# Layer 0 starts with two groups of value columns for each slice of x instead of one

## The chip, the core and the metric

The kernel runs on one core of a Trainium2 chip. The time is that of one execution on the device in microseconds (us); a measurement gives the median of several. Lines such as L313 are lines of the kernel before.

## What is computed

Two layers of a block on x, 256 positions by 2048 features, in float32. Each layer projects x to ten groups of columns (convolution, six hgrn heads, six retention heads), mixes along the sequence in three ways, projects back, adds and normalises, then does a squared-ReLU feed-forward of width 8192, adds and normalises again.

```python
for l in range(DEPTH):
    proj = jnp.einsum('btd,de->bte', x, w_in[l])
    ca, cg, hq, hf, hi, hg, rq, rk, rv, rg = jnp.split(proj, split_idx, axis=-1)
    y_conv = conv_mixer(ca, cg, ...)
    y_hgrn = hgrn2_mixer(hq, hf, hi, hg, lower_bounds[l], hgrn_norm_g[l])
    y_ret = retention_mixer(rq, rk, rv, rg, positions, ...)
    mix = jnp.concatenate([y_conv, y_hgrn, y_ret], axis=-1)
    x = layer_norm(DEEPNORM_ALPHA * x + mix @ w_out[l], ...)
    f = jnp.square(jax.nn.relu(x @ w_ff1[l]))
    x = layer_norm(DEEPNORM_ALPHA * x + f @ w_ff2[l], ...)
```

The values are the columns hi and rv, 768 each: 1536 columns, that is three groups of 512. Heads 0 to 3 of hgrn read group 0; hgrn heads 4 and 5 read the first half of group 1, retention heads 0 and 1 the second half; the other retention heads read group 2.

## The kernel before, in words

Every large product is made of float32r matmuls on numbers split in two: a cast to float32r (the high part) and the remainder. Weights come from HBM in float32 into one of three `raw` buffers of 1 MB (`load2`, L268). ScalarE (ACT) casts half a buffer into a `wp` tile (L288), VectorE (DVE) writes the remainder beside it (L291). Such a half is a *unit*; there are six `wp` tiles. x goes the same way into the `act` tiles (L388, L390).

There are two kinds of product. `xstat` holds a 128x128 block of x in TensorE (PE) and streams 512 weight columns past it (L313): for each of eight slices i of 256 features, two tiles t of 128 positions, with six matmuls each (two blocks of 128 features, three products: high by high, high by remainder, remainder by high). A group so takes 96 matmuls in two PSUM accumulators. `wstat` holds weights and streams x (L363, L365), 256 output columns at a time, in two loads of 1 MB. There are four accumulators, `mm`. The value groups go through `xstat`, the other columns of the input projection through `wstat`, in the order of the table `ORDER`.

Nothing runs in the order in which the code stands. Each operation is handed to a planner (`Plan`) with its engine, a cost, what it reads and writes, and urgency. The planner lays all engines out by its own costs and then emits each engine's fixed sequence. The large products keep their order on PE (`main`); the casts keep the order of the units (chain `hi`), the remainders theirs (chain `lo`), and the weight loads theirs on SyncE's queue (chain `dma`). The rest (products of the heads on PE, evictions, 124 multiply-adds of the convolution on DVE) is put between. On the chip each engine takes its sequence strictly in order, and an instruction that waits holds up what stands behind it. A load into a `raw` buffer waits until the part of the buffer that it writes has been read by the cast and the remainder.

Layer 0 begins with eleven warm-up matmuls on zeros (L449). Then value group 0 runs while x itself arrives: `first_x` loads a transposed slice of x (0.25 MB for each of the first two, then 0.5 MB for two slices together), and splits it. `fine` says into how many parts the load of a 1 MB weight buffer is cut: four for the first, two for the others. After the fourth slice `setup` loads the constants (`cst`), a mask and the positions, and works out tables on DVE and ACT: the lower bounds (`lbs`, L494 to L514), the mask's cast (L460), and the angles (L465 to L484). Then come the `wstat` products from `ORDER`. Value group 1 stands ahead of ("hf", 2), the gates of the third pair of hgrn heads, and value group 2 ahead of ("rq", 0), the first retention pair. The score products of an hgrn pair are L588, seven steps of L604, and L645; the convolution's transposes are L803, its ACT steps L815 and L824, and the product that follows them on DVE L828.

Of the kernel before, what the change touches and what calls it, by code (L numbers as in the profile page):

```python
# [202 lines left out]
def block_kernel(ctx: ExitStack, tc: tile.TileContext, a: dict, out: bass.AP):  # L203
# [7 lines left out]
    def ring(name, n, shape, dt=F32, p=pool):  # L211
        return Ring([p.tile(list(shape), dt, name=f"{name}{i}") for i in range(n)])
# [8 lines left out]
    mm = ring("mm", 4, [P, W], F32, psum)  # L221
# [43 lines left out]
    def load2(src, parts=1):  # L265

        raw, n = raws.buf(), 2048 // parts
        ops = [op("DMA", 2.92 / parts, lambda f=f: nc.sync.dma_start(  # L268
            out=raw.t[:, f * n:(f + 1) * n], in_=src[:, f * n:(f + 1) * n]), w=[(raw, f * n // 1024 if parts == 2
                                                                                else f if parts > 1 else None)],  # L270
            chain="dma") for f in range(parts)]
        return raw, ops, parts

    def unit(ld, i, pool_lo=False):

        u = Unit()
        raw, dmas, parts = ld
        u.w, u.parts = wps.buf(), max(parts // 2, 1)
        n = 1024 // u.parts
        u.ops = dmas[i * u.parts:(i + 1) * u.parts] if parts > 1 else dmas  # L280
        u.ops = [(o, 4.5) for o in u.ops]
        for f in range(u.parts):
            sl, pt = slice(f * n, (f + 1) * n), f if u.parts > 1 else None
            rs = slice(1024 * i + f * n, 1024 * i + (f + 1) * n)
            rk = (raw, None if parts == 1 else i * u.parts + f)

            def hi(sl=sl, rs=rs):
                S.copy(out=u.w.t[:, 0, sl], in_=raw.t[:, rs])  # L288

            def lo(sl=sl, rs=rs):  # L290
                (G if pool_lo else V).tensor_tensor(out=u.w.t[:, 1, sl], in0=raw.t[:, rs],  # L291
                                                    in1=u.w.t[:, 0, sl].bitcast(F32), op=ALU.subtract)

            eng, cost = ("POOL", 2.35) if pool_lo else ("DVE", dve(n))
            u.ops += [(op("ACT", act(n), hi, r=[rk], w=[(u.w, pt)], chain="hi"), 2.5),
                      (op(eng, cost, lo, r=[rk], w=[(u.w, pt)], chain="lo" + eng), 1.3)]
        return u
# [6 lines left out]
    def mmx(u, ps, xT, i, t):  # L304

        parts = u.parts
        for kbs in ((0, 1),) if parts == 1 else ((0,), (1,)):
            def fn(kbs=kbs):
                w = u.w.t.rearrange("p s (k c) -> p s k c", k=2)
                for kb in kbs:  # L310
                    k = 2 * i + kb
                    for n, (xs, ws) in enumerate(((0, 0), (0, 1), (1, 0))):
                        nc.tensor.matmul(  # L313
                            ps.t, lhsT=xT[k // 4].t[:, xs, k % 4, t * P:(t + 1) * P], rhs=w[:, ws, kb, :],
                            start=(k == 0 and n == 0), stop=(k == KB - 1 and n == 2))

            w = u.w if parts == 1 else (u.w, kbs[0])
            needed(u, plan.main(3 * len(kbs) * 0.2161, fn, [w, (xT[i // 2], i if (i // 2, parts) == (0, 2) else t)],
                                [ps]))

    def xstat(src, xT, done, head=0, tail=0, before=None, pool_lo=(), fine={}):

        ps = [mm.buf(), mm.buf()]
        order = [(i, t) for i in range(8) for t in range(2)]
        if tail:
            order = order[:16 - 2 * tail] + [(i, t) for t in range(2) for i in range(8 - tail, 8)]
        if head:
            order = [(i, 0) for i in range(head)] + [(0, 1), (1, 1), (2, 1)]  # L330
            for i in range(head, 8):
                order += [(i, 0), (i - head + 3, 1)]
            order += [(i, 1) for i in range(8) if (i, 1) not in order]
        us = {}
        for i, t in order:
            if t == 0:
                if before is not None:
                    before(i)
                if i % 2 == 0:
                    ld = load2(src[i // 2], fine.get(i, 1))  # L340
                us[i] = unit(ld, i % 2, i in pool_lo)
            mmx(us[i], ps[t], xT, i, t)
            if i == 7:
                done(t, ps[t])

    def wstat(src, xT, dst=None):

# [76 lines left out]
    xT = [acts.buf() for _ in range(4)]  # L424
# [521 lines left out]
    for l in range(DEPTH):  # L946
        mixT = [acts.buf() for _ in range(4)]
        vt = []

        def vgroup(g, **kw):  # L950
            tl = []
            vt.append(tl)

            def done(t, ps):
                v = r2.buf()
                op("ACT", act(W, ps=True), lambda: S.copy(out=v.t, in_=ps.t), r=[ps], w=[v], floor=1.5)
                tl.append(v)

            xstat(a["wv"][l, g], xT, done, **kw)

        if l == 0:
            def before(i):
                first_x(i)
                if i == 3:
                    setup((plan.last["PE"],))

            vgroup(0, before=before, fine={0: 4, 2: 2, 4: 2, 6: 2})
            whole(xT[0])
        else:
            vgroup(0, head=HEAD, pool_lo=POOL_LO)  # L970
            norm.rest()
        pairs, gates = {}, {}
        for i, (kind, p) in enumerate(ORDER):
            if (kind, p) == ("hf", 2):
                vgroup(1)
            if (kind, p) == ("rq", 0):
                vgroup(2)
            if kind in ("hf", "rq"):
                pair = pairbufs.buf()
                pairs[kind[0], p] = pair  # L980
            dst = None
            if kind in ("rq", "rk"):
                dst = (pairs["r", p], "Q" if kind == "rq" else "K", pv(pairs["r", p], 0 if kind == "rq" else 1))
            pr = wstat(a["wp"][l, i], xT, dst)
            if l == 0 and i == 1:
                op("DMA", 6.0, lambda: nc.sync.dma_start(out=x_nat.t, in_=a["x"].rearrange("(t p) d -> p t d", p=P)),
                   w=[x_nat], after=(plan.last["PE"],))
            if kind == "hf":
                hgrn_gates(l, p, pr, pair)
            elif kind == "hq":  # L990
                Qv = pv(pair, 2)
                op("ACT", act(W), lambda Qv=Qv, pr=pr: S.activation(out=Qv(), in_=pr.t, func=AF.Sigmoid), r=[pr],
                   w=[(pair, "Q")])
                op("DVE", dve(W), lambda Qv=Qv, pr=pr: V.tensor_tensor(out=Qv(), in0=pr.t, in1=Qv(), op=ALU.mult),
                   r=[pr], w=[(pair, "Q")])
            elif kind == "hg":
                gate = r2.buf()
                op("ACT", act(W), lambda gate=gate, pr=pr: S.activation(out=gate.t, in_=pr.t, func=AF.Sigmoid),
                   r=[pr], w=[gate])
                hgrn(l, p, pairs["h", p], gate, vt, mixT)  # L1000
            elif kind in ("cg", "ca"):
                def uv(p=p):
                    return u_t.t[:, 2 * p:2 * p + 2, CONVW - 1:]

                uk = [(u_t, 2 * p), (u_t, 2 * p + 1)]
                if kind == "cg":
                    op("ACT", act(W), lambda uv=uv, pr=pr: S.activation(out=uv(), in_=bl(pr.t, 2), func=AF.Sigmoid),
                       r=[pr], w=uk)
                else:
                    op("DVE", dve(W), lambda uv=uv, pr=pr: V.tensor_tensor(out=uv(), in0=bl(pr.t, 2), in1=uv(),  # L1010
                                                                           op=ALU.mult), r=[pr], w=uk)
                    if p == 0:
                        accs = [r2.buf(), r2.buf()]
                    conv_taps(l, accs[p], 2 * p)
                    if p == 1:
                        conv(l, accs, mixT)
            elif kind == "rg":
                gate = r2.buf()
                op("ACT", act(W), lambda gate=gate, pr=pr: S.activation(out=gate.t, in_=pr.t, func=AF.Sigmoid),
                   r=[pr], w=[gate])  # L1020
                op("DVE", dve(W), lambda gate=gate, pr=pr: V.tensor_tensor(out=gate.t, in0=pr.t, in1=gate.t,
                                                                           op=ALU.mult), r=[pr], w=[gate])
                ret(l, p, pairs["r", p], gate, vt, mixT)
# [8 lines left out]
        xT = norm.xT  # L1032
# [37 lines left out]
        xT = norm.xT  # L1070
# [107 lines left out]
```

## Time and profile before

| what | value |
|---|---|
| median of three executions | 2340.0 us (2339.7 to 2341.8) |
| the profiled execution's own time | 2341.0 us |
| its span, first to last instruction | 2339.2 us |
| PE, DVE, ACT busy | 99%, 64%, 45% of the span |
| first matmul of value group 0, first matmul of the first `wstat` | 5.49 us, 32.32 us |

Times in rows of the timeline are us from the first instruction: start, duration, engine, line, operation, out<-in, how many in a row, and in brackets the idle time before with what ended it. In a list of groups a row ends with busy us, mean ns of one, and the idle time ahead of it. A row of a DMA group gives its count, the KB of one and the median us from issue to landing. Matmuls overlap: one is shown as busy for about 0.5 us, and the next begins before it ends.

### The profile page before, as it was taken

What the parts mean: (1) busy time and instruction counts of PE and PEld (TensorE: products, weight loads), DVE (VectorE), ACT (ScalarE), POOL (GpSimd) and SP (SyncE); (2) the same over time, 40 slices, a digit from 0 to 9 for tenths busy, and PEclk for the clock granted to TensorE, in tenths of its full rate; (3) what the DMA queues carried; (4) which work ended last, traced back from release to release, by engine and by line L of the source; (5) the groups of instructions that cost most, each with busy time, mean ns of one, the idle gap of its engine ahead of it and who ended that gap; (6) DMA issues with size and microseconds to landing.
All of it is one profiled execution on the core that took longest, in us unless ns stands there. A gap on an engine that the chain in (4) does not pass through costs nothing.

```text
span 2339.2 us, 29616 instructions
## 1 busy us (share of the span) xinstructions
PE 2320.4 (99%) x12067; PEld 1974.0 (84%) x12067; DVE 1504.0 (64%) x2046; ACT 1054.0 (45%) x1334; POOL 65.0 (3%) x66
## 2 busy tenths in 40 slices
PE   9999999999999999999999999999999999999998
PEld 7888888788888888888888888887888888888886
DVE  6997666665565565565579976656655655655655
ACT  6445444454344344344444455444543444443442
POOL 0000000100000000000000000101000000000000
PEclk9999999999999999999999999999999999999999
DMA  8544566465555555556454445564555555555563
GB/s 299 181 162 162 171 198 207 162 207 188 190 189 189 198 180 198 188 190 205 167 205 162 163 162 174 189 218 159 205 198 185 193 187 191 185 193 198 181 229 113
DMA packets 67705, 439.90 MB, mean 188 GB/s; under 512 B 7664, under 2 KB 7920, under 8 KB 16624
## 3 DMA queue, kind: packets, MB, share of 16 engines
q1 hardware_dynamic: 67568, 438.01, 55.0%
q8 instruction: 94, 1.54, 0.2%
q14 instruction: 43, 0.35, 0.0%
HBM read 432.74 MB, written 2.10 MB: 186 GB/s over the span
## 4 chain that ended last, share of the span: by engine, by line
PE 98%; DVE 1%; DMA 0%; ACT 0%; issue 0%; SPq 0%; DVEq 0%
PE mm L313 44%; PE mm L363 33%; PE mm L365 17%; PE aux L604 2%; PE aux L399 1%; DVE x_nat L889 0%; DMA raw<-in_wv 0%; PE aux L550 0%; PE aux L552 0%; PE aux L588 0%; PE aux L548 0%; PE aux L717 0%; DVE x_nat L883 0%; ACT r L913 0%; DVE sm L861 0%
## 5 line engine op out<-in xcount | busy, mean ns | idle before, releaser
L291 DVE TENSOR_TENSOR wp<-raw,wp 128x1024 fp32r<-128x1024 f32 (+1 forms) x796 | 970.9, 1221 | 602.4 <-ACT wp L288 600.6
L288 ACT CAST wp<-raw 128x1024 fp32r<-128x1024 f32 (+1 forms) x802 | 842.4, 1052 | 819.0 <-PE mm L313 561.7
L363 PE MATMUL mm<-act,wp 128*128 128x512 f32 x3328 | 1180.8, 399 | 0.0
L313 PE MATMUL mm<-wp,act 128*128 128x512 f32 x4608 | 1061.1, 390 | 3.9 <-ACT wp L288 1.7
L313 PEld LDWEIGHTS mm<-wp,act 128*128 128x128 f32 x4608 | 861.1, 188 | 185.4 <-ACT wp L288 2.9
L365 PE MATMUL mm<-act,wp 128*128 128x256 f32 x3328 | 933.2, 280 | 0.0
L363 PEld LDWEIGHTS mm<-act,wp 128*128 128x128 f32 x3328 | 625.4, 188 | 151.5
L365 PEld LDWEIGHTS mm<-act,wp 128*128 128x128 f32 x3328 | 628.4, 189 | 0.5
L372 ACT COPY r<-mm 128x256 f32<-128x256 f32 x208 | 77.9, 375 | 369.6 <-PE mm L365 369.3
L375 DVE TENSOR_TENSOR r<-mm,r 128x256 f32<-128x256 f32 x184 | 78.1, 424 | 146.2 <-ACT r L372 145.9
L791 DVE SCALAR_TENSOR_TENSOR r<-u_t,cst,r 128x256 f32<-128x256 f32 x240 | 102.1, 479 | 0.0
L407 POOL TENSOR_TENSOR sm<-sm,mhalf 128x4 f32<-128x4 f32 (+1 forms) x24 | 30.4, 1266 | 2252.5 <-DVE sm L873 1589.4
L388 ACT CAST act<-r 128x512 fp32r<-128x512 f32 x82 | 51.5, 628 | 21.7 <-DVE r L1049 16.2
L390 DVE TENSOR_TENSOR act<-r,act 128x512 fp32r<-128x512 f32 x82 | 57.9, 706 | 0.0
L604 PEld LDWEIGHTS aux<-pair 128*128 128x128 f32 x336 | 42.4, 191 | 2.6
L1049 DVE SCALAR_TENSOR_TENSOR r<-r 128x512 f32<-128x512 f32 x60 | 41.6, 693 | 2.1
L604 PE MATMUL aux<-pair 128*128 128x64 f32 x336 | 42.0, 267 | 0.0
L940 DVE TENSOR_TENSOR x_nat<-x_nat,mm 128x512 f32<-128x512 f32 x48 | 30.8, 681 | 12.7 <-PE mm L313 12.7
L938 DVE SCALAR_TENSOR_TENSOR x_nat<-x_nat,mm 128x512 f32<-128x512 f32 x32 | 20.6, 680 | 11.7 <-PE mm L313 11.7
L889 DVE SCALAR_TENSOR_TENSOR x_nat<-x_nat,sm,r 128x512 f32<-128x512 f32 x26 | 24.3, 989 | 0.0
L609 DVE COPY_PREDICATED r<-maskl,aux 128x256 f32<-128x256 uint8 x42 | 21.9, 521 | 0.0
L375 DVE TENSOR_TENSOR pair<-mm,r 128x256 f32<-128x256 f32 x24 | 10.2, 423 | 17.8 <-ACT r L372 17.8
(115 smaller groups left out, 513.4 us busy)
## 6 DMA issues: line engine op xcount, KB each, us to landing
raw<-in_w SPq DMA_DIRECT2D x248, 1024.0 KB, 4.8
raw<-in_wp SPq DMA_DIRECT2D x88, 1024.0 KB, 4.8
raw<-in_wo SPq DMA_DIRECT2D x32, 1024.0 KB, 4.8
raw<-in_wv SPq DMA_DIRECT2D x20, 1024.0 KB, 4.8
raw<-in_w1x SPq DMA_DIRECT2D x8, 1024.0 KB, 4.8
raw<-in_wv SPq DMA_DIRECT2D x6, 512.0 KB, 6.0
pair<-pair SPq DMA_DIRECT2D x24, 128.0 KB, 2.3
x_nat<-in_x SPq DMA_DIRECT2D x1, 2048.0 KB, 9.4
```

The lines of the kernel that those rows point to most:

```text
L288: S.copy(out=u.w.t[:, 0, sl], in_=raw.t[:, rs])
L291: (G if pool_lo else V).tensor_tensor(out=u.w.t[:, 1, sl], in0=raw.t[:, rs], in1=u.w.t[:, 0, sl].bitcast(F32), op=ALU.subtract)
L313: nc.tensor.matmul(ps.t, lhsT=xT[k // 4].t[:, xs, k % 4, t * P:(t + 1) * P], rhs=w[:, ws, kb, :], start=(k == 0 and n == 0), stop=(k == KB ...
L363: nc.tensor.matmul(pv, lhsT=w[:, 0, kb, :], rhs=xt[:, :, k % 4, :], start=(k == 0), stop=False)
L365: nc.tensor.matmul(pv[:, 0, :], lhsT=w[:, 1, kb, :], rhs=xt[:, 0, k % 4, :], start=False, stop=(k == KB - 1))
L372: S.copy(out=low.t, in_=ps.t[:, T:])
L375: V.tensor_tensor(out=dst[2]()[:, b * T:(b + 1) * T], in0=ps.t[:, 0:T], in1=low.t, op=ALU.add)
L388: op("ACT", act(n, ps=ps), lambda: S.copy(out=x.t[:, 0, blks, cols], in_=bl(src(), nb)), r=r, w=[(x, part)], **kw)
L390: op("DVE", dve(n), lambda: V.tensor_tensor(out=x.t[:, 1, blks, cols], in0=bl(src(), nb), in1=x.t[:, 0, blks, cols].bitcast(F32), op=ALU.s ...
L604: nc.tensor.matmul(ps.t[:, b * 64:(b + 1) * 64], lhsT=Kt()[:, b * P:(b + 1) * P], rhs=rhs, start=True, stop=True)
L791: V.scalar_tensor_tensor(out=d, in0=src, scalar=cw[:, l, b, j:j + 1], in1=d, op0=ALU.mult, op1=ALU.add)
L1049: op("DVE", dve(W), lambda f=f, r=r: V.scalar_tensor_tensor(out=f.t, in0=r.t, scalar=0.0, in1=r.t, op0=ALU.max, op1=ALU.mult), r=[r], w=[f ...
```

## The change

In layer 0 the first two value groups run together. For each slice of x, `xstat2` does the twelve matmuls of group 0 and then the twelve of group 1, in four accumulators. Each group has its own loads; the first of group 0 is cut into four as before, the first of group 1 and the second of group 0 into two, and the others are whole. Group 1's place ahead of ("hf", 2) is left out in layer 0. Layer 1 is unchanged, as is the amount of work.

```diff
+    def xstat2(srcs, xT, dones, before, fine):
+
+        ps = [[mm.buf(), mm.buf()] for _ in srcs]
+        us = {}
+        for i in range(8):
+            before(i)
+            for n, src in enumerate(srcs):
+                if i % 2 == 0:
+                    us[n, "ld"] = load2(src[i // 2], fine.get((n, i), 1))
+                us[n, i] = unit(us[n, "ld"], i % 2)
+                for t in range(2):
+                    mmx(us[n, i], ps[n][t], xT, i, t)
+                    if i == 7:
+                        dones[n](t, ps[n][t])
...
-            vgroup(0, before=before, fine={0: 4, 2: 2, 4: 2, 6: 2})
+            xstat2([a["wv"][l, 0], a["wv"][l, 1]], xT, [vdone(), vdone()], before, {(0, 0): 4, (1, 0): 2, (0, 2): 2})
...
-            if (kind, p) == ("hf", 2):
+            if (kind, p) == ("hf", 2) and l:
                 vgroup(1)
```

`vdone` is the old eviction of `vgroup`, made a function of its own. The planner makes other sequences of this. SyncE's queue at the very start, before (`raw` numbers are the three buffers, `in_xt` is x, `in_wv` the value weights, `in_wp` those of the first `wstat`):

```order
L434 DMA raw_61<-in_xt 128x512
L268 DMA raw_62<-in_wv 128x512 x4
L434 DMA raw_63<-in_xt 128x512
L434 DMA raw_61<-in_xt 128x1024
L268 DMA raw_62<-in_wv 128x1024 x2
L434 DMA raw_63<-in_xt 128x1024
L268 DMA raw_61<-in_wv 128x1024 x2
L434 DMA raw_62<-in_xt 128x1024
L422 DMA cst<-in_pack 128x710
L268 DMA raw_63<-in_wv 128x1024 x2
L268 DMA raw_61<-in_wp 128x2048
```

And of the change, whose line numbers are 15 higher from there on:

```order
L449 DMA raw_61<-in_xt 128x512
L268 DMA raw_62<-in_wv 128x512 x4
L268 DMA raw_63<-in_wv 128x1024 x2
L449 DMA raw_61<-in_xt 128x512
L449 DMA raw_62<-in_xt 128x1024
L268 DMA raw_63<-in_wv 128x1024 x2
L268 DMA raw_61<-in_wv 128x2048
L449 DMA raw_62<-in_xt 128x1024
L268 DMA raw_63<-in_wv 128x2048
L437 DMA cst<-in_pack 128x710
L268 DMA raw_62<-in_wv 128x2048
L449 DMA raw_61<-in_xt 128x1024
```

The second slice of x moved behind group 1's first load and into the buffer of the first slice. The constants have five value loads of 1 MB ahead of them instead of three.

DVE in the same stage, before. `sm` and `lbs` are the tables of the lower bounds, `act` is x, `wp` a unit (the ring is 64 to 69):

```order
L291 TENSOR_TENSOR wp_68<-raw_61,wp_68 128x1024
L291 TENSOR_TENSOR wp_69<-raw_61,wp_69 128x1024
L494 TENSOR_TENSOR sm_95<-cst 128x6
L496 TENSOR_TENSOR sm_95<-cst,sm_95 128x6 x2
L390 TENSOR_TENSOR act_75<-raw_62,act_75 128x1024
L505 RECIPROCAL sm_95<-sm_95 128x12
```

And of the change, the rows around the tables:

```order
L291 TENSOR_TENSOR wp_64<-raw_63,wp_64 128x1024
L405 TENSOR_TENSOR act_74<-raw_62,act_74 128x1024
L291 TENSOR_TENSOR wp_65<-raw_61,wp_65 128x1024
L509 TENSOR_TENSOR sm_95<-cst 128x6
L511 TENSOR_TENSOR sm_95<-cst,sm_95 128x6
L511 TENSOR_TENSOR sm_95<-cst,sm_95 128x6
L291 TENSOR_TENSOR wp_66<-raw_63,wp_66 128x1024
L520 RECIPROCAL sm_95<-sm_95 128x12
L521 TENSOR_TENSOR sm_95<-sm_95 128x12
```

The tables now stand between the remainders of the value groups' fourth and fifth slices; before, six of eight units were ahead of them. The angles (L480 to L490 of the change) follow behind the sixth slice and ahead of the seventh; before, they stood behind the units of the first `wstat`.

PE at the end of the third hgrn pair, before. `pair` holds the pair's queries and keys, `mm` are the accumulators of value group 2:

```order
L604 MATMUL aux_107<-pair_70 128x64 x4
L313 MATMUL mm_103<-wp_66,act_72 128x512 x6
L604 MATMUL aux_108<-pair_70 128x64 x4
L313 MATMUL mm_104<-wp_66,act_72 128x512 x6
L604 MATMUL aux_105<-pair_70 128x64 x4
L313 MATMUL mm_103<-wp_67,act_72 128x512 x6
L604 MATMUL aux_106<-pair_70 128x64 x4
L313 MATMUL mm_104<-wp_67,act_72 128x512 x6
L604 MATMUL aux_107<-pair_70 128x64 x4
L313 MATMUL mm_103<-wp_68,act_73 128x512 x6
L645 MATMUL aux_108<-pair_70 128x128 x2
```

And of the change (L619 is L604, L660 is L645, L414 are the convolution's second transposes):

```order
L414 MATMUL aux_106<-cst,r_1_81 128x128 x4
L619 MATMUL aux_107<-pair_70 128x64 x4
L313 MATMUL mm_104<-wp_68,act_73 128x512 x6
L619 MATMUL aux_105<-pair_70 128x64 x4
L313 MATMUL mm_103<-wp_69,act_73 128x512 x6
L619 MATMUL aux_108<-pair_70 128x64 x4
L313 MATMUL mm_104<-wp_69,act_73 128x512 x6
L619 MATMUL aux_107<-pair_70 128x64 x4
L313 MATMUL mm_103<-wp_64,act_74 128x512 x6
L660 MATMUL aux_105<-pair_70 128x128 x2
```

The pair's last product (L645, L660) moved from the third slice of value group 2 into its fifth, and the convolution's transposes, which stood ahead of the pair, now stand between its steps. From the end of value group 2 on, PE's sequence is the same to the end of the program.

More of the change, by code (lines that the diff above doesn't have):

```diff
@@ L948, in block_kernel, with vdone @@
         vt = []
-        def vgroup(g, **kw):
+        def vdone():
             tl = []
@@ L957, in done, with vgroup @@
                 tl.append(v)
-            xstat(a["wv"][l, g], xT, done, **kw)
+            return done
+        def vgroup(g, **kw):
+            xstat(a["wv"][l, g], xT, vdone(), **kw)
         if l == 0:
```

## Prediction

> **What bounds the kernel now.** First the page: what share TensorE has of the span, and which chain ends last.
>
> ```profile
> span 2339.2 us, 29616 instructions
> PE 2320.4 (99%) x12067; PEld 1974.0 (84%) x12067; DVE 1504.0 (64%) x2046; ACT 1054.0 (45%) x1334; POOL 65.0 (3%) x66
> PE 98%; DVE 1%; DMA 0%; ACT 0%; issue 0%; SPq 0%; DVEq 0%
> ```
>
> PE is busy 99% and carries 98% of the chain. The change removes no matmul, so it can only win what PE loses by waiting. The waits of PE over the whole span (who waited, for whom, us, times, longest) say where that is:
>
> ```profile
> PE aux L399 <- DVE x_nat L889: 3.5, 3, 1.2
> PE mm L313 <- ACT wp L288: 1.7, 1, 1.7
> ...
> PE mm L313 <- DVE wp L291: 1.0, 2, 0.8
> ```
>
> L399 waits at the layer norms, which the change leaves alone. The two L313 rows are the first value group. PE's timeline from the start, and one row of a later stage:
>
> ```profile
> 5.49 2.18 PE L313 MATMUL mm<-wp,act 128*128 128x512 f32 x4
> 7.90 4.87 PE L313 MATMUL mm<-wp,act 128*128 128x512 f32 x20 [0.23 <-DVE wp L291]
> 14.48 0.51 PE L313 MATMUL mm<-wp,act 128*128 128x512 f32 x1 [1.72 <-ACT wp L288]
> 15.75 16.74 PE L313 MATMUL mm<-wp,act 128*128 128x512 f32 x71 [0.76 <-DVE wp L291]
> 32.32 0.39 PE L363 MATMUL mm<-act,wp 128*128 128x512 f32 x1
> ...
> 559.79 74.28 PE L313 MATMUL mm<-wp,act 128*128 128x512 f32 x327
> ```
>
> Unhindered, one L313 takes 74.28 / 327 = 0.227 us. The first group is 96 of them: 21.8 us of work, from 5.49 to 32.32 = 26.83 us. It loses 5.0 us, more than the waits show, since a busy bar of 0.5 us hides a gap of 0.27 us. By place: 7.90 - 5.49 - 4 x 0.227 = 1.5 us before the second k-block of the first unit; 14.48 - 7.90 - 20 x 0.227 = 2.0; 15.75 - 14.48 - 0.23 = 1.0; the rest, 0.5, among the 71. So 5.0 us (0.21% of 2340) is the ceiling of any gain, and the first 1.5 us stay, since the first unit's loads are unchanged: at most 3.5 us can be won.
>
> **What PE waits for there.** SyncE's issues and the starts on ACT that a landing released:
>
> ```profile
> 1.17 1.84 SPq L268 DMA_DIRECT2D raw<-in_wv  x4
> 3.05 2.61 SPq L434 DMA_DIRECT2D raw<-in_xt  x2
> 3.96 0.62 ACT L388 CAST act<-raw 128x512 fp32r<-128x512 f32 x1 [1.96 <-DMA raw<-in_xt]
> 7.51 1.27 ACT L288 CAST wp<-raw 128x512 fp32r<-128x512 f32 x2 [0.40 <-DMA raw<-in_wv]
> 7.87 1.99 SPq L268 DMA_DIRECT2D raw<-in_wv  x2
> 10.05 1.05 ACT L388 CAST act<-raw 128x1024 fp32r<-128x1024 f32 x1 [0.63 <-DMA raw<-in_xt]
> 13.39 1.04 ACT L288 CAST wp<-raw 128x1024 fp32r<-128x1024 f32 x1 [2.29 <-DMA raw<-in_wv]
> ```
>
> 1 MB had landed by 7.51 (a quarter MB of x, three quarters of weights), 2 MB by 10.05: 0.39 MB/us. The third weight unit landed at 13.39, because its buffer came free only at 7.87. Two limits: the rate, and three raw buffers.
>
> **The change, new order, step by step.** These durations price it (busy us, mean ns; then landings):
>
> ```profile
> L291 DVE TENSOR_TENSOR wp<-raw,wp 128x1024 fp32r<-128x1024 f32 x20 | 24.0, 1222 | 9.2 <-ACT wp L288 8.9 <-issue 0.2
> L291 DVE TENSOR_TENSOR wp<-raw,wp 128x512 fp32r<-128x512 f32 x4 | 2.7, 692 | 1.5 <-ACT wp L288 1.4
> L288 ACT CAST wp<-raw 128x1024 fp32r<-128x1024 f32 x21 | 21.7, 1048 | 12.1 <-DMA raw<-in_wv 5.1 <-DMA raw<-in_wp 4.2 <-issue 2.9
> L288 ACT CAST wp<-raw 128x512 fp32r<-128x512 f32 x4 | 2.5, 619 | 1.7 <-DMA raw<-in_wv 1.7
> raw<-in_wp SPq DMA_DIRECT2D x9, 1024.0 KB, 6.6
> raw<-in_wv SPq DMA_DIRECT2D x6, 512.0 KB, 6.0
> cst<-in_pack SPq DMA_DIRECT2D x1, 355.0 KB, 5.8
> r<-in_maskl SPq DMA_DIRECT2D x1, 224.0 KB, 8.3
> r<-in_pos SPq DMA_DIRECT2D x1, 128.0 KB, 8.9
> raw<-in_wv SPq DMA_DIRECT2D x20, 1024.0 KB, 4.8
> ```
>
> The last row is the page's, of loads that mostly stand alone; the others are of the first 60 us. Casts and remainders of x take the same as those of weights of their size.
>
> 1. First unit of the new group. PE ends the first unit at 7.90 + 8 x 0.227 = 9.7. The new half MB stands fourth in the queue and completes 1.75 MB: 7.51 + 0.75 / 0.39 = 9.4, taken as 9.5. Cast on ACT to 10.55, remainder on DVE to 11.8. The first matmul needs the cast, the second the remainder: waits of 0.9 and 1.0, end 14.35. With 0.29 MB/us (the whole run-up, 1.75 MB from the first start on ACT, 3.96, to 10.05) it lands at 9.9, 0.4 us more.
> 2. Second slice of x. It is now issued behind 1 MB of the new group, and split behind that group's second unit: ACT until 13.5 (two 512 casts, one 1024, one 512), DVE until 15.1. PE reaches the matmul that needs its remainder at 14.8: 0.3 us.
> 3. Second load of the new group (1 MB). Its buffer is the one of that slice of x: issued at 15.15. It lands after 4.8 (alone) to 6.6 us (behind others); half a MB is ahead, so 21.2. Remainder ready at 23.5; PE wants it at 20.1 + 2.73 + 0.23 = 23.1: 0.4 us.
> 4. The constants. SyncE issues them behind the third load of the old group, whose buffer is free once the fourth unit's remainder is done, 23.5 + 1.22 = 24.7. Landing 25.1 + 5.8 = 30.9. DVE's three small operations (0.17 each) that read them now stand ahead of the remainder of the fifth slice's first unit, so that is done at 31.4 + 1.22 = 32.65. PE, at 26.0 after step 3 and two units later at 31.45, wants it one matmul on, at 31.7: 0.95 us. The nine table operations that follow push the next remainder to 35.8: 0.4 us.
>
> ```profile
> 23.80 0.23 DVE L505 RECIPROCAL sm<-sm 128x12 f32<-128x12 f32 x1 [0.26 <-ACT sm L501]
> 25.57 0.17 DVE L514 TENSOR_SCALAR lbs<-lbs 128x6 f32<-128x6 f32 x1
> 32.66 0.39 DVE L460 CAST maskl<-r 128x448 uint8<-128x448 f32 x1
> 35.23 0.29 DVE L465 CAST r<-r 128x256 f32<-128x256 int32 x1
> 38.44 0.29 DVE L475 TENSOR_SCALAR r<-r 128x256 f32<-128x256 f32 x1
> ```
>
> 5. The angles. Nine tables are 25.74 - 23.80 = 1.94 us, the angles 38.73 - 35.23 = 3.5, the mask cast before them 0.4. They had PE work already covered by units in store (the first wstat); now they stand ahead of the remainder of the seventh slice. DVE is then full from 30.9: remainders end at 32.65, 35.8, 37.05, 39.5, x's last quarter at 38.3 between, the angles at 43.4, the seventh slice at 44.65. PE, at 35.8 + 2.5 = 38.3 after step 4, wants it two units and a matmul on, at 44.0: 0.65 us, and 0.1 for its partner.
> 6. Accumulators: four instead of two; the first wstat reuses the first, whose eviction has one unit (2.7 us) of time. Nothing. The issue of more or other DMAs costs nothing: SyncE's queue has the same 468 rows.
>
> Sum after: 1.5 + 1.9 + 0.3 + 0.4 + 1.35 + 0.75 = 6.2 us lost, against 5.0: +1.2 us. What it saves, the 3.5 us of waits for the third unit and x, really goes; the second group's own weights take their place.
>
> 7. The place left, before the third hgrn pair. No PE row waits there, so taking 96 matmuls out gives 21.8 us, what their share of the start adds unhindered. But DVE loses cover:
>
> ```profile
> 60.00:210.00 150.00, 150.00 (x895) 132.09 (x894) 138.24 (x284) 72.30 (x111) 6.55 (x6) 1.00 0.49 166
> 210.00:262.00 52.00, 52.00 (x300) 45.32 (x299) 33.80 (x61) 21.81 (x30) 1.02 (x1) 1.00 0.48 161
> ```
>
> DVE is busy 138.24 of 150 us (the third number with a count). Without the group's eight remainders (8 x 1.22 = 9.8) it has 128.5 us of work in the 128.2 that are left. Its 11.8 us of idle time, waits for ACT and PE, stay in part, so up to 12 us must go past that stage, where DVE has 18 us free. In the order the third pair's last score product has 246 matmuls of L313 ahead of it and had 222: 24 x 0.227 = 5.4 us later. That leaves 6.6 us of lag at worst, 0 at best. I take 0.3: the nearest row, DVE at 92% beside a PE that waits for nothing, shows no loss.
>
> Together +1.5 us. The profiled execution took 2341.0 (span 2339.2 and 1.8 around), so such a one would take 2342.5; it was 1.0 above the median, so the median goes from 2340.0 to **2341.5**. A measurement can tell about 0.2%, 4.7 us.
>
> **A rule of the Trainium skill against these rows.** "DMA: Bandwidth & Descriptors", section "Anatomy of one DMA — SWDGE (gpsimd) path", gives about 2.0 us plus bytes over 436 GB/s (fitted on GpSimd's path). By it step 1's half MB would land near 7.4, step 1's waits would vanish and the sum would be about 2339.6. The row at 10.05 (the half MB of x whose issue ends at 5.66, for which that rule gives about 8.5) speaks against it, so the trace's rate stands.
>
> **Rivals.**
> - All lands in time (loads at the 4.8 row's pace, constants early): nothing is lost beyond the first 1.5 us: 2340.0 - 3.5 = 2336.5. For: each wait above but step 1's is under 1 us, of a landing known to 1 us. Against: step 1's half MB would have to land by 9.7 - 1.05 - 1.22 = 7.4, when by the rows 1 MB is there, not 1.75. Chance 0.09. A gain over 4.7 us is nearly the whole ceiling, of which 1.5 stay: 0.02 for what no row shows.
> - The constants are late: DVE, in order, stands at its first read of them with the remainders of the slices 5 to 7 behind it, and is full until 44.65, so each us of delay is a us of PE. It decides from a landing at 34 (25.1 + 8.9, what the position's load of this stage takes): +3.1 on the 1.5, 2344.6 and more. Slower by 0.2%: chance 0.10 with later raw buffers counted.
> - DVE falls behind at the third hgrn pair: PE stands at its score products, +5: 2346.5. It decides from 3.5 us of lag left there. For: 128.5 in 128.2. Against: the order gives 5.4 us, and the stage behind has room. Chance 0.05.
> - The clock. The eleven warm-up products (same columns) run at half speed:
>
> ```profile
> 1.17 4.87 PE L449 MATMUL aux<-wz 128*128 128x512 bf16 x11 [1.17 <-DVE wz L444]
> ```
>
> 0.44 us each; a fall back to that for 15 products would cost 3.2 us: 2344.7. The 1.72 us wait at 14.48 caused none (the 71 after it average 0.23), and the new waits are shorter. Chance 0.02. "TensorE: Matmul & The Clock Gate", Part 1, of the Trainium skill puts the idle window that halves the clock at about 3.4 us; no wait here is so long, before or as forecast.
>
> **How the numbers follow.** The forecast has 0.72: from -1.3 (steps 3 to 5 at nothing) to +4.5 (landings 1 us later, 2 us of step 7). The range adds most of the late constants above and part of the first rival below: 2337.5 to 2346.0. Faster by over 0.2%: 0.02. Slower: 0.10 + 0.05 (the clock's case just misses): 0.15. Same: 0.83.
>
> **What would show it.** After: first L363 near 55.4 (32.32 + 21.8 + 1.2); a wait of L313 of about 1 us for L288 at 10 and one for L291 at 11; no wait of 1.7; short waits for L291 near 32, 36 and 44; no PE wait from 60 to 260. Wrong: first L363 before 53 or after 58, or PE waits for L604, L588 or L399 after 180.

## The result, and the profile after

The change takes 2344.23 us (median of 21, 2342.60 to 2345.32), before 2340.65 (21, 2339.40 to 2342.50). The medians lie 3.6 us apart. The estimate of the ratio is 1.0012, 95% interval 1.0007 to 1.0018: slower by 2.8 us (1.6 to 4.2), which is within 0.2%. The prediction said +1.5 us, and had 2341.5 from a base of 2340.0, the median of three; the longer series puts the base 0.65 us higher. The rest of its error is a cost taken too small.

The profiled execution took 2343.55 us. Its page, first part and chain by engine:

```profile
span 2341.8 us, 29606 instructions
PE 2322.9 (99%) x12067; PEld 1974.9 (84%) x12067; DVE 1503.0 (64%) x2046; ACT 1052.7 (45%) x1334; POOL 63.5 (3%) x66
...
PE 96%; DVE 1%; DMA 1%; ACT 1%; issue 0%; SPq 0%; DVEq 0%; ACTq 0%
```

The span is 2.6 us longer, PE's busy time 2.5 us, with the same 12067 matmuls. So PE's busy time alone does not say where the loss is: a short gap hides in it, and so do slow matmuls. PE left 2% of the chain to DMA and ACT. PE's waits over the whole span:

```profile
PE aux L414 <- DVE x_nat L904: 3.5, 3, 1.2
PE mm L313 <- DVE wp L291: 1.7, 4, 0.8
...
PE mm L313 <- ACT wp L288: 0.9, 1, 0.9
```

The 1.7 us wait for a cast is gone. In its place stand one of 0.9 for a cast and four for remainders. The timeline of PE places them:

```profile
5.53 3.72 PE L313 MATMUL mm<-wp,act 128*128 128x512 f32 x12
10.15 0.50 PE L313 MATMUL mm<-wp,act 128*128 128x512 f32 x1 [0.90 <-ACT wp L288]
11.41 20.99 PE L313 MATMUL mm<-wp,act 128*128 128x512 f32 x84 [0.76 <-DVE wp L291]
32.70 3.04 PE L313 MATMUL mm<-wp,act 128*128 128x512 f32 x12 [0.30 <-DVE wp L291]
36.11 11.43 PE L313 MATMUL mm<-wp,act 128*128 128x512 f32 x48 [0.37 <-DVE wp L291]
47.83 8.23 PE L313 MATMUL mm<-wp,act 128*128 128x512 f32 x35 [0.29 <-DVE wp L291]
55.90 0.39 PE L378 MATMUL mm<-act,wp 128*128 128x512 f32 x1
```

192 matmuls at 0.227 are 43.6 us; from 5.53 to 55.90 are 50.37, so 6.8 us are lost (forecast 6.2). The first `wstat` matmul stands at 55.90. Before, with the 21.8 us of the second group added, it would stand at 32.32 + 21.8 = 54.1. So 1.8 of the 2.6 us are lost ahead of it.

One loss of this stage shows in no wait. The windows of the same execution (start and end, us; busy us and count of PE, PEld, DVE, ACT, POOL; the clock; DMA's share; GB/s):

```profile
9.00:12.40 3.40, 1.74 (x7) 1.03 (x6) 2.27 (x3) 3.35 (x5) 0.00 (x0) 1.00 0.66 262
12.40:15.60 3.20, 3.20 (x9) 2.47 (x9) 3.03 (x4) 1.89 (x3) 0.00 (x0) 0.52 0.70 221
```

From 12.4 to 15.6 PE is "busy" throughout, but the granted clock is 0.52 and 9 matmuls run in 3.2 us, where 14 would have at 0.227: 1.2 us or more are lost there (about 1.6 over the whole of the slow stretch, in which matmuls start 0.43 us apart). And the late stage, whose DVE had 18 us free before:

```profile
210.00:262.00 52.00, 52.00 (x307) 45.41 (x306) 41.36 (x80) 29.90 (x53) 3.05 (x6) 1.00 0.48 162
```

DVE's busy time in it went from 33.80 to 41.36 us: its work did slide back past the third hgrn pair, and PE still waits for nothing there.

### The profile page after: what moved, and what is told of

It is laid out like the page before. It is cut to its first block, busy times and chain, and to the rows that moved or that the text cites. A ratio compares the mean times of both kernels' runs of the same rounds, so it can differ in the third digit from the quotient of the medians.

```text
span 2341.8 us, 29606 instructions
## 1 busy us (share of the span) xinstructions
PE 2322.9 (99%) x12067; PEld 1974.9 (84%) x12067; DVE 1503.0 (64%) x2046; ACT 1052.7 (45%) x1334; POOL 63.5 (3%) x66
## 3 DMA queue, kind: packets, MB, share of 16 engines
q8 instruction: 94, 1.54, 0.3%
## 4 chain that ended last, share of the span: by engine, by line
PE 96%; DVE 1%; DMA 1%; ACT 1%; issue 0%; SPq 0%; DVEq 0%; ACTq 0%
PE mm L313 43%; PE mm L378 33%; PE mm L380 17%; PE aux L619 2%; DMA raw<-in_wv 1%; PE aux L414 1%; DVE x_nat L904 0%; ACT wp L288 0%; PE aux L567 0%; PE aux L565 0%; PE aux L603 0%; PE aux L563 0%; PE aux L732 0%; DVE x_nat L898 0%; DVE wp L291 0%
## 5 line engine op out<-in xcount | busy, mean ns | idle before, releaser
L619 PEld LDWEIGHTS aux<-pair 128*128 128x128 f32 x336 | 42.0, 191 | 2.3
L619 PE MATMUL aux<-pair 128*128 128x64 f32 x336 | 42.0, 267 | 0.0
L955 DVE TENSOR_TENSOR x_nat<-x_nat,mm 128x512 f32<-128x512 f32 x48 | 30.9, 681 | 12.7 <-PE mm L313 12.7
```

What stands on the lines that cost most here:

```text
L619: nc.tensor.matmul(ps.t[:, b * 64:(b + 1) * 64], lhsT=Kt()[:, b * P:(b + 1) * P], rhs=rhs, start=True, stop=True)
```

## The experiments

All make the whole computation. Each ran 11 times beside 33 runs of the kernel before on the same chip (medians 2340.89, 2340.96 and 2340.93 in the three sets). The edits are on the change; where an edit touches the call of `xstat2`, only its last argument is shown. "First `wstat`" is the start of its first matmul on PE; 54.1 is what before corresponds to.

**First set: which part loses?** The theory was the prediction's: the start loses, late, because the constants arrive late and DVE works out its tables ahead of the remainders. Rivals: the place that the second group left; and the early loss, by the slow clock and the first waits.

*The second group at the start, but behind the first* instead of beside it:

```diff
-            xstat2([a["wv"][l, 0], a["wv"][l, 1]], xT, [vdone(), vdone()], before, {(0, 0): 4, (1, 0): 2, (0, 2): 2})
+            vgroup(0, before=before, fine={0: 4, 2: 2, 4: 2, 6: 2})
             whole(xT[0])
+            vgroup(1)
```

> Group 1 leaves its later place as in the change, but runs behind group 0 and not beside it, so the start is that of the kernel before. If the interleaved start costs the time (my theory): first wstat matmul at 32.3 + 21.8 = 54.1 us, and the whole within 0.7 us of the kernel before. If the place that group 1 left costs it (DVE without cover before the third hgrn pair): first wstat matmul at 54.1 as well, but the whole slower by about 2.8 us, as the change is.

Measured 2341.30, ratio 0.9999 (0.9990 to 1.0008). PE's timeline:

```profile
14.97 0.50 PE L313 MATMUL mm<-wp,act 128*128 128x512 f32 x1 [1.16 <-ACT wp L288]
16.23 38.15 PE L313 MATMUL mm<-wp,act 128*128 128x512 f32 x167 [0.76 <-DVE wp L291]
54.22 0.39 PE L378 MATMUL mm<-act,wp 128*128 128x512 f32 x1
```

It waits early, like before, and then never again. The place left is empty here too, and the time is that of before: the rival of the place left falls. The loss is in the interleaved start, with its loads cut as they are there.

*Six more matmuls on zeros* between the two groups' first units, into an accumulator that nobody reads, so that PE has work while it waits there (`fill` issues them):

```diff
+FILL = 6
...
+                if (n, i) == (1, 0):
+                    plan.main(0.2161 * FILL, fill, [wz], [wps_])
```

> The change, with six dummy matmuls on zeros (1.3 us) on PE where it waits for the first unit of group 1. In the change's trace the granted clock falls to 0.52 from 12.4 to 15.6 us, which costs 1.5 us there. Theory A (landings and DVE's sequence set the end of the start, the clock only eats slack): the clock stays at 1.00, yet the first wstat matmul stays at 55.4 to 55.9 us, with longer waits for DVE at 32, 35 and 47; the whole within 0.5 us of the change. Theory B (the clock is the cost): first wstat matmul at 54.4 us, the whole 1.5 us faster than the change. If the clock falls all the same, the dummies do not keep it up.

*The constants and tables behind both groups:*

```diff
-                if i == 3:
-                    setup((plan.last["PE"],))
...
             whole(xT[0])
+            setup((plan.last["PE"],))
```

> The change, with the constants, mask, positions and their tables asked for only behind both groups. The wait before the first unit of group 1 and the fall of the clock stay. Theory A: the waits for DVE near 32, 35 and 47 us (0.57 + 0.64 + 0.56 of lost time) go, first wstat matmul at 54.1 to 54.6 us, the whole 1.3 to 1.8 us faster than the change (about 1 us slower than the kernel before). Theory B: those waits are not what sets the end; no more than 0.5 us is won.

*Both*, the two edits above, unchanged:

> The change with both: dummies in the first wait and the constants behind both groups. Theory A: the two only pay together: first wstat matmul at 52.5 to 53.4 us (lost: 1.9 before the first unit of group 1, 1.0 within it, 0.5 to 1.4 at the second load of group 1), the whole 0.7 to 1.6 us faster than the kernel before and 3 us faster than the change. Theory B: no more than what the dummies alone give, 1.5 us faster than the change.

Measured: filling 2344.21 (1.0011, 1.0002 to 1.0020), constants late 2342.97 (1.0006, 0.9997 to 1.0015), both 2343.91 (1.0011, 1.0003 to 1.0020). The last missed what was expected of it, 3 us under the change. The granted clock was 1.00 from 9 to 15.6 us in both profiles with the filling, and yet the two medians are within 0.4 us of the change's 2344.23: a full clock early does not pay by itself. In the trace of both edits together PE waits again later (0.76 at 24.32, 1.01 and 0.76 at 33.58 and 34.84, 0.65 at 49.37), and the first `wstat` stands at 57.46. (The profiled execution of the filling alone was the fastest of its eleven, 2341.78, with its first `wstat` at 54.25, so its rows are not typical.) Taking constants and tables out of the way wins about 1.3 us on the medians, and with the filling none that shows; why the two together do worse than the second alone was not settled. PE's timeline with the constants late:

```profile
11.94 20.97 PE L313 MATMUL mm<-wp,act 128*128 128x512 f32 x84 [0.76 <-DVE wp L291]
33.66 21.85 PE L313 MATMUL mm<-wp,act 128*128 128x512 f32 x95 [0.75 <-DVE wp L291]
55.35 0.39 PE L378 MATMUL mm<-act,wp 128*128 128x512 f32 x1
```

The wait near 33 is still there, longer even, with no table ahead of that remainder: the load was issued at 25.38, its cast began when it had landed, at 31.30, and the remainder followed at 32.38. So the constants alone were not its cause, and the theory fell in that part. The two later waits are gone here. At the first of them the remainder is no earlier than in the change (it starts at 34.89 and 34.83), but PE is 0.96 us later; at the second it starts 0.8 us earlier (45.75 and 46.55). The first `wstat` stands at 55.35, where 54.1 to 54.6 was expected.

**A new theory: the raw buffers.** SyncE's queue in the change says when each load could be asked for:

```profile
11.38 3.27 SPq L268 DMA_DIRECT2D raw<-in_wv  x3
...
24.36 0.33 SPq L268 DMA_DIRECT2D raw<-in_wv  x1
...
37.22 1.46 SPq L268 DMA_DIRECT2D raw<-in_wv  x2
```

ACT's timeline says when their halves could be cast:

```profile
30.26 1.05 ACT L288 CAST wp<-raw 128x1024 fp32r<-128x1024 f32 x1 [5.47 <-DMA raw<-in_wv]
...
33.63 2.00 ACT L288 CAST wp<-raw 128x1024 fp32r<-128x1024 f32 x2 [0.69 <-DMA raw<-in_wv]
...
42.13 1.05 ACT L288 CAST wp<-raw 128x1024 fp32r<-128x1024 f32 x1 [4.61 <-DMA raw<-in_wv]
...
45.47 4.85 ACT L288 CAST wp<-raw 128x1024 fp32r<-128x1024 f32 x5 [0.15 <-DMA raw<-in_wv]
```

and DVE's timeline when the remainders behind them ran:

```profile
31.07 0.17 DVE L509 TENSOR_TENSOR sm<-cst 128x6 f32<-128x6 f32 x1 [4.47 <-DMA cst<-in_pack]
...
31.43 1.22 DVE L291 TENSOR_TENSOR wp<-raw,wp 128x1024 fp32r<-128x1024 f32 x1
...
34.83 2.36 DVE L291 TENSOR_TENSOR wp<-raw,wp 128x1024 fp32r<-128x1024 f32 x2
...
42.88 0.29 DVE L490 TENSOR_SCALAR r<-r 128x256 f32<-128x256 f32 x1
43.22 1.23 DVE L291 TENSOR_TENSOR wp<-raw,wp 128x1024 fp32r<-128x1024 f32 x1
...
46.55 2.36 DVE L291 TENSOR_TENSOR wp<-raw,wp 128x1024 fp32r<-128x1024 f32 x2 [0.91 <-ACT wp L288]
```

The load for slices 5 and 6 is issued at 24.36, when both halves of its buffer have been read, and its first half is cast from 30.26. That cast ends at 31.31, and the remainder starts at 31.43: the three small operations ahead of it held it up by 0.1 us at most. The remainder at 34.83, on which PE's wait at 36.11 hangs, needed a cast that ran from 33.63, after a landing, to about 34.7; the last table ahead of it frees DVE at 34.8, which is later by 0.1 us. At the seventh slice the cast ends at 43.18 and the angles at 43.17: without the angles the remainder could have come no earlier. The remainder at 46.55, on which PE's wait at 47.83 hangs, was preceded by 0.91 us of idle time on DVE, for a cast that followed a landing; that load was issued at 38.35, when the last slices of x had been split and their buffer was free. So each of these remainders came within 0.15 us of what its load allowed. The chain that the profile follows back from 47.83 does run through the tables, but only by that 0.1 us at 34.8, so this trace alone cannot choose between loads and tables; taking each away can. The loads of one pair of slices follow the pair before by 37.22 - 24.36 = 12.9 us, and PE needs 4 units x 12 x 0.227 = 10.9 us for a pair.

A load of 1 MB in one piece waits for the whole buffer. In halves, its first half may come as soon as the buffer's first half has been read. Before, all loads of the first group behind the first were in halves. In the change one of the two groups' eight is in quarters, two are in halves, and five are whole. The theory says: halves win back the loss, whatever is early; rival: the early waits.

**Second set.** *Every later load of both groups in halves:*

```diff
-{(0, 0): 4, (1, 0): 2, (0, 2): 2}
+{(0, 0): 4, (1, 0): 2, **{(n, i): 2 for n in range(2) for i in (2, 4, 6)}}
```

> The change, with every load of the two groups cut into halves, so that a half buffer is asked for as soon as its own half is read; constants where the change has them. In the last four kernels neither the clock nor the constants' place moved the median by more than about 1 us, and their traces show the third pair of slices' weights issued at 24 to 25 us and landing near 31, whatever came before: theory A now is that the three raw buffers, each held from issue to the reading of its second half, set the pace (12 us for a pair of slices, where PE needs 10.9). Theory A: these issues come 1.2 to 2.4 us earlier, PE's waits between 30 and 50 us go, first wstat matmul at 53.6 to 54.4 us, the whole 1.3 to 2 us faster than the change. Theory B (DVE's sequence with the constants in it sets the pace): first wstat matmul stays at 55 to 56 us, the whole within 0.5 us of the change.

*Early part alone:* the second group's first load in quarters, the rest as in the change.

```diff
-{(0, 0): 4, (1, 0): 2, (0, 2): 2}
+{(0, 0): 4, (1, 0): 4, (0, 2): 2}
```

> The change, with only the first load of group 1 cut into four and not two: its first quarter lands near 8.4 us and not 9.0, and the half-size cast and remainder take 0.62 and 0.69 and not 1.05 and 1.22 us. PE's waits at its first unit fall from 0.9 + 1.0 to about 0.5, and the clock stays up. Theory A (the raw buffers set the pace): the 2.5 to 3 us won at 15 us are lost again by 50 us, first wstat matmul at 55 to 56, the whole within 0.7 us of the change. Theory C (the early waits and the clock are the cost): first wstat matmul near 53, the whole 2.5 us faster than the change.

Halves 2341.29 (2340.53 to 2342.60; ratio 1.0002, 0.9993 to 1.0011), quarters alone 2344.69 (2343.71 to 2345.81; 1.0014, 1.0005 to 1.0023). The two series, on the same chip, do not touch. Halves won more than was expected (1.3 to 2 us under the change; 2.9 against its 2344.23). PE's timeline with halves, the last of its waits in brackets:

```profile
12.39 41.70 PE L313 MATMUL mm<-wp,act 128*128 128x512 f32 x179 [0.76 <-DVE wp L291]
53.94 0.39 PE L378 MATMUL mm<-act,wp 128*128 128x512 f32 x1
```

179 matmuls without a wait. SyncE's queue and ACT's timeline of this run show why:

```profile
18.21 5.96 SPq L268 DMA_DIRECT2D raw<-in_wv  x2
```

```profile
24.75 1.05 ACT L288 CAST wp<-raw 128x1024 fp32r<-128x1024 f32 x1 [0.25 <-DMA raw<-in_wv]
...
36.66 1.06 ACT L288 CAST wp<-raw 128x1024 fp32r<-128x1024 f32 x1 [0.81 <-DMA raw<-in_wv]
```

The first half of the load for slices 5 and 6 is issued at 18.21 instead of 24.36, and cast at 24.75 instead of 30.26; that of slices 7 and 8 is cast at 36.66 instead of 42.13. Each comes 5.5 us sooner. The planner now puts the fifth slice's first remainder ahead of the tables, while the next remainders still stand behind them and the seventh slice's behind the angles, and PE waits for none. That other order on DVE could be a rival to the halves themselves; the runs below that leave the tables out, or the order as it was, answer it. With quarters alone:

```profile
9.70 0.50 PE L313 MATMUL mm<-wp,act 128*128 128x512 f32 x1 [0.35 <-ACT wp L288]
10.42 8.62 PE L313 MATMUL mm<-wp,act 128*128 128x512 f32 x36 [0.22 <-DVE wp L291]
...
33.49 3.02 PE L313 MATMUL mm<-wp,act 128*128 128x512 f32 x12 [0.84 <-DVE wp L291]
36.90 19.84 PE L313 MATMUL mm<-wp,act 128*128 128x512 f32 x83 [0.39 <-DVE wp L291]
56.57 0.39 PE L378 MATMUL mm<-act,wp 128*128 128x512 f32 x1
```

It is ahead of the change by 0.45 us at the second group's first cast and by 1 us at its remainder, its clock stays at 1.00, and later it stands at 33.49 and 36.90, behind the change (32.70 and 36.11). The early win is paid back: the buffers, not PE, set the pace.

*A buffer of its own for x*, so that the weights keep three (ring `r2` went from 11 buffers to 9 to make room; a fourth raw buffer of 1 MB was not tried):

```diff
+    xraw = ring("xraw", 1, [P, 1024])
...
-    r2 = ring("r2_", 11, [P, W])
+    r2 = ring("r2_", 9, [P, W])
...
-        raw = raws.buf()
+        raw = xraw.buf()
```

> The change, with a buffer of half a MB for x alone, so that the three raw buffers hold weights only (paid for with two of the eleven 128x512 tiles of the r2 ring, which may cost something in the middle of the layer). Theory A (raw buffers set the pace): a load of weights no longer waits for x to be split, the first load of slices 5 and 6 is issued before 21 us and not at 24.4, no PE wait from 20 to 50 us, first wstat matmul at 53.4 to 54.2 us (the first waits and the fall of the clock, 4.4 us, stay). Theory B: first wstat matmul at 55 to 56 us. The whole: faster than the change by 1.5 to 2.5 us under A if the smaller ring costs nothing.

Measured 2345.16 (1.0018, 1.0009 to 1.0027), slower. The time that was expected did not come, and SyncE's queue says why:

```profile
4.82 9.99 SPq L450 DMA_DIRECT2D xraw<-in_xt  x2
14.86 1.37 SPq L269 DMA_DIRECT2D raw<-in_wv  x3
```

The third load of x waits in the queue for its only buffer, and the weight loads stand behind it until 14.86 (11.38 in the change), though their buffer is free. The issue that was expected did come: the first load for slices 5 and 6 stands at 20.67 instead of 24.36, and from 22.82 on PE runs 143 matmuls without a wait. But PE was itself late by then (1.76 us for a cast at 21.56), and its clock was at 0.51 from 23.3 to 26.8. So the run tells what a blocked queue costs; it agrees with the theory in the late part and cannot price the buffer.

*Quarters, halves and the constants late together:*

```diff
-                if i == 3:
-                    setup((plan.last["PE"],))
...
-{(0, 0): 4, (1, 0): 2, (0, 2): 2}
+{(0, 0): 4, (1, 0): 4, **{(n, i): 2 for n in range(2) for i in (2, 4, 6)}}
             whole(xT[0])
+            setup((plan.last["PE"],))
```

> The change, with the first load of group 1 cut into four, all others of the two groups into halves, and the constants behind both groups. If the loss is what the three marks of the trace say (2.2 us at the first unit of group 1, 1.5 us of half clock after it, 1.8 us of waits from 30 to 50 us), all three shrink: first wstat matmul at 50.6 to 52 us, no fall of the clock, the whole 2 to 3.5 us faster than the kernel before (ratio 0.9985 to 0.9991). If the loads as such set the end (5 MB of weights and x at the start's rate), the waits come back later: first wstat matmul at 54 or more, the whole no faster than the kernel before.

Measured 2340.14 (2338.73 to 2340.98; 0.9996, 0.9987 to 1.0004), level with before. The first `wstat` came as expected (51.56, in the fastest of the eleven); the whole, expected 2 to 3.5 us faster than before, did not. Neither this run nor the one with the constants late alone has a table among the two groups' remainders. They differ in quarters and halves, and their series lie apart, 2340.98 at most against 2341.88 at least, 2.8 us on the medians (on two chips, where before agrees within 0.1). So what the halves win is not DVE's order.

**Third set.** *The same with the constants where the change has them*, to price those alone:

```diff
-{(0, 0): 4, (1, 0): 2, (0, 2): 2}
+{(0, 0): 4, (1, 0): 4, **{(n, i): 2 for n in range(2) for i in (2, 4, 6)}}
```

> The change, with the first load of group 1 in quarters and all later loads in halves; constants where the change has them. Apart from the constants it is the kernel that was 0.8 us faster than the kernel before. Theory A (with the raw buffers asked for by halves the constants' place matters little): first wstat matmul at 51.5 to 53 us, the whole within 1 us of the kernel before. If the constants' tables hold up DVE as steps 4 and 5 had it: first wstat matmul at 53.5 to 54.5, about 2 us slower than with the constants behind both groups.

Measured 2340.75 (2340.33 to 2341.74; 0.9999, 0.9990 to 1.0007). With halves the constants cost 2340.75 - 2340.14 = 0.6 us, of two sets' medians, less than either series spreads. The first `wstat` stands at 53.19, between what the two theories gave it.

*Turned round: one more load made whole*, the second of the first group:

```diff
-{(0, 0): 4, (1, 0): 2, (0, 2): 2}
+{(0, 0): 4, (1, 0): 2}
```

> The change, with group 0's second load whole and not in halves: the cure of the halves turned round. Theory A: this load is asked for at 13.7 us (both halves of its buffer read) and not at 11.4, and lands whole near 19.5 and not by halves at 14.8 and 18.4; PE, which wants its remainder at 20, waits 1 to 2 us, and the later loads move by as much: first wstat matmul at 56.5 to 58 us, the whole 1 to 2 us slower than the change. If the buffers do not set the pace: within 0.5 us of the change.

*The change itself once more*, on that chip:

> The change itself, beside the three others on their chip: 2 to 4 us slower than the kernel before; in its trace the first wstat matmul within 1.5 us of 55.9, the loads for slices 5 and 6 issued at 24 to 25.5 us. A fall of the clock after the first unit of group 1 may or may not be there.

Measured: one more whole load 2345.44 (1.0018, 1.0009 to 1.0026), first `wstat` at 57.29, with DVE's order around the tables that of the change; the change 2344.45 (2343.76 to 2345.76; 1.0015, 1.0007 to 1.0024). Quarters and halves lose nothing, the change's mix +3.5 us on the medians, one more whole load another 1.0. The change and the run with quarters and halves do not touch either (2341.74 against 2343.76). PE's timeline of the change in this execution:

```profile
10.30 0.50 PE L313 MATMUL mm<-wp,act 128*128 128x512 f32 x1 [1.41 <-ACT wp L288]
11.56 11.49 PE L313 MATMUL mm<-wp,act 128*128 128x512 f32 x48 [0.76 <-DVE wp L291]
23.81 8.66 PE L313 MATMUL mm<-wp,act 128*128 128x512 f32 x36 [0.76 <-DVE wp L291]
33.30 3.01 PE L313 MATMUL mm<-wp,act 128*128 128x512 f32 x12 [0.83 <-DVE wp L291]
36.72 11.34 PE L313 MATMUL mm<-wp,act 128*128 128x512 f32 x48 [0.41 <-DVE wp L291]
48.65 8.23 PE L313 MATMUL mm<-wp,act 128*128 128x512 f32 x35 [0.58 <-DVE wp L291]
56.71 0.39 PE L378 MATMUL mm<-act,wp 128*128 128x512 f32 x1
```

and its windows where the other execution had the slow clock:

```profile
9.00:12.40 3.40, 1.34 (x5) 0.90 (x6) 2.12 (x3) 3.19 (x5) 0.00 (x0) 1.00 0.67 268
12.40:15.60 3.20, 3.20 (x16) 2.57 (x15) 3.19 (x4) 1.84 (x3) 0.00 (x0) 1.00 0.69 216
```

At full clock it has a wait of 0.76 at 23.81 that the other did not have, and 0.83, 0.41 and 0.58 against 0.30, 0.37 and 0.29 later. What the clock cost in one execution, the loads cost in the other.

*A better version:* quarters, halves, constants late, and in `xstat2` the two products with the cast weights ahead of the one with the remainder, for both blocks of a unit:

```diff
-                for kb in kbs:
+                terms = [(kb, xs, ws) for kb in kbs for xs, ws in ((0, 0), (0, 1), (1, 0))]
+                if hifirst:
+                    terms.sort(key=lambda v: v[2])
```

> Quarters, halves and the constants behind both groups, and in both groups the matmuls that need only the cast weights ahead of those that need the remainder (four matmuls, 0.9 us, of cover for each remainder). Expected: the wait for a remainder near 18.7 us (0.7 shown, 1.0 lost) shrinks to 0.3 or less, first wstat matmul at 50.6 to 51.3 us, the whole 1.2 to 2 us faster than the kernel before (ratio 0.9991 to 0.9995). If waits only move to the next load: first wstat matmul at 51.6 again.

Measured 2339.01 (2337.87 to 2340.48; 0.9991, 0.9982 to 1.0000), 1.9 us under before, as expected, and 1.1 under the run without the sorting (of another set on the same chip): the best of all, at the edge of what the interval tells from before. PE's timeline:

```profile
8.13 5.55 PE L315 MATMUL mm<-wp,act 128*128 128x512 f32 x22 [0.86 <-ACT wp L288]
13.94 38.83 PE L315 MATMUL mm<-wp,act 128*128 128x512 f32 x167 [0.26 <-DVE act L408]
52.60 0.39 PE L381 MATMUL mm<-act,wp 128*128 128x512 f32 x1
```

No wait for a remainder of the weights is left in this execution; one for a cast and one for a remainder of x are. The first `wstat` came later than expected, 52.60 against 50.6 to 51.3, and later than the 51.56 of the run without the sorting, whose profiled execution was its fastest. So where in the program the 1.1 us are won is not shown.

## Why the prediction held, and where it did not

- **Step 1, the new half MB.** Right: cast and remainder forecast at 10.55 and 11.8, the matmuls that need them found at 10.15 and 11.41. The half MB was there at 9.05, where 0.39 MB/us gave 9.4. (It is the sixth load in the queue and not the fourth; the 1.75 MB are right.) By the formula of "DMA: Bandwidth & Descriptors" in the Trainium skill, section "Anatomy of one DMA — SWDGE (gpsimd) path", as the prediction applied it, there would have been no wait here. The trace has one of 0.90, so the measured rate was the better guide.
- **Steps 2 and 3, x and the second load.** No wait stands at 14.8 or 23.1 in the first execution; PE was late itself, by the slow clock. In the second, the wait of step 3 is there: 0.76 before 23.81 (1.0 with the gap that the busy bar hides), forecast 0.4.
- **Steps 4 and 5, the late waits.** The times were right: the constants read at 31.07 (forecast landing 30.9), the remainder behind them done at 32.65 (32.65), the seventh slice's at 44.45 (44.65). The cause was not, and this is the step that failed. It priced what stands ahead of the remainders on DVE (tables and angles), and gave no price to the loads that these remainders need, which are now whole and land just as late. It had named the three raw buffers as a limit, and counted "later raw buffers" into the chance of a rival, but put no time to them. So it would have had nothing left to lose with the tables away, where a run with the constants late still waits 0.75 us at 33.66; and it would have kept the seventh slice's waits with halves, where the angles still stand ahead of it and none is left. It also missed the wait at 47.83, for the seventh slice's second unit: it had 0.1 us there, for DVE's sequence, and its load came late. Halves are worth 2.9 us (2344.23 against 2341.29), the constants out of the way 1.3, and with the loads cut 0.6; the two steps together had 1.35 + 0.75 = 2.1 us, put down to the tables.
- **Step 6, accumulators.** Nothing stood for them, as said.
- **Step 7, the place left.** 0.3 was taken; the run with the second group behind the first costs nothing that shows in its median. DVE's lag was real and free.
- **The sum.** +1.5 against +2.8 (1.6 to 4.2): the right sign, the size just under the interval. PE's timelines, at 0.227 for each matmul, say where. In the first execution 2.9 us are lost up to 11.41 (forecast 3.4), and 3.9 from there to the first `wstat` (forecast 2.8), of which about 1.6 are the slow clock. In the second, at full clock, it is 3.25 up to 11.56 and 4.5 behind: there the terms of steps 3 to 5, those of the loads, were the ones that were too small. That the first execution's 6.8 comes so near the forecast's 6.2 is in part luck, since the clock stood in the sum at nothing.
- **The rivals.** "All in time" and the third hgrn pair: not seen. The clock, given 0.02, did come in one of the two profiled executions of the change, but without a price of its own in the end: the other, at full clock, is as slow (2343.76 against 2343.55), the loads taking the time instead.

Still open: of the 2.6 us of the profiled pair, some 0.5 appear only between 266 and 343 us, where no wait of PE shows; the run with the second group behind the first shows about as much there and ends level. Its cause was not looked for. Nor is it known how much of the spread of an execution (about 1 us) comes from landings.

## What to carry to other kernels

Where loads run through few buffers, read from the queue when each load is issued, not only when it lands: a load in one piece waits for the whole of its buffer, one in halves for half, and here that decided 3 us that looked like waits for a vector engine. A wait saved early is worth nothing while such a loop sets the pace behind it: try the suspected cause alone before adding up waits.

## What the hardware showed that was not expected

- The granted clock fell to 0.52 for 3.2 us right behind waits of 0.90 and 0.76 us, with PE busy 1.74 of the 3.4 us before; in another execution of the same kernel PE was busy only 1.34 of 3.4 us, behind waits of 1.41 and 0.76, and the clock stayed at 1.00. By the rule of "TensorE: Matmul & The Clock Gate", Part 1, of the Trainium skill, an idle window of about 3.4 us, neither should have slowed; the measurement decides.
- What may tell the two apart is where the waits fall on a grid of time. The trace's clock records have the rise at 5.70 in the first execution, the fall 2 x 3.41 us later, at 12.52, and the next rise after another 3.41. Counted in steps of 3.41 from the rise, PE was busy 1.75 us in the step ahead of the fall. In the second execution the rise is at 3.87, and the same waits are shared by two steps, busy 2.00 and 2.66. The two other falls that the kept traces have ahead of the program's end (constants late, and the buffer for x) follow steps busy 1.54 and 1.00; but one step of 1.76, in the run with filling and constants late, had no fall behind it. This was read from the traces afterwards, and no run tests it.
- A load of 1 MB with the constants and another 1 MB load issued within 1.2 us behind it took 5.9 us from issue to the start of its cast (24.36 to 30.26), and the same with the constants out of the queue (25.38 to 31.30); the page's row has 4.8 to the landing for those that mostly stand alone.
